# A hybrid SSM, attention and MoE block: w_out loaded during attention, and token tile 0 computed behind its split

## The chip, the cores and the metric

The kernel runs on one core of one Trainium2 chip, and its measure is the device time of one execution in microseconds. Three runs of the kernel before gave 1213.77, 1214.08 and 1216.22 us: the median is 1214.08. One more execution was profiled. It took 1210.29 us.

## The reference

The block works on 1024 tokens of 1024 channels in float32. A root-mean-square norm and one input projection give u (512 channels), q, k and v (8 heads of 64). An S5 state-space mixer turns u into y_ssm; stick-breaking attention turns q, k and v into y_att. What bears on this case comes behind both:

```
mixed = concat([rms_norm(y_ssm, g_ssm_out), rms_norm(y_att, g_attn_out)], axis=-1)   # 512 + 512 channels
x = x + mixed @ w_out                       # w_out: 1024 x 1024
h2 = rms_norm(x, g_ffn)
x = x + hierarchical_moe(h2, ...)           # 4 groups of 8 experts: the best group, its two best experts
```

rms_norm(x, g) is x / sqrt(mean(x²) + 1e-6) · g over the last axis. The MoE has 32 experts, each with a gate, an up and a down matrix (SwiGLU), 1024 x 512 or 512 x 1024.

## The kernel before, in words

**Engines and order.** Each engine (PE, DVE, ACT, POOL) and each DMA queue (SP's, ACT's, POOL's) works through its instructions in the order in which they stand; semaphores hold an instruction until what it needs is there. Outside the MoE, the scheduler of the tile framework sets that order. Buffers lie in pools on a left and a right stack of the on-chip memory, and a pool that is opened later reuses the space of one that was closed; an instruction that writes there waits for the last reader of what lay there.

**Float32 products in three passes.** A float32 operand is split into a high and a low part: `split` (L86 to L88) copies the high part on ACT (L87) and subtracts on DVE (L88). `split_mm` (L90 to L93) adds hi·hi, hi·lo and lo·hi in one PSUM bank. PSUM has 8 banks, under three tags: 3 `acc`, 2 `tr` (transposes) and 3 `m`.

**Attention.** The 8 heads go in four pairs, 8 query blocks of 128 each. For a head and a block, `att_a` makes the scores on PE (L688 to L692), a sigmoid on ACT (L693, into sb), 1 − x on POOL (L694, into bb) and a scan on DVE (L697); `att_b` transposes (L708) and copies (L712 on ACT, L714 on DVE); `att_c` multiplies with v (L721) and copies the result into q_t (L723, ACT), which by then is called oT. The scores of a pair's last block are 1024 wide, so the scans show where a pair ends and the next begins. zT, in the space of yT, holds y_ssm, transposed.

**Out projection.** Behind the attention come the small loads: gcat (the gains of both norms, SP), wr (the router's weights, L778 and L779, on ACT's queue), gpc (g_ffn, L781) and br_b (the router's bias, L784 and L785); L782 multiplies wr by gpc on DVE. Then:
- w_out in 8 row blocks of 128. Each is loaded into one of two buffers `wor` (L794, SP), scaled by gcat into wh on ACT (L795), and its low part wl made on DVE (L796). The pair is `wo[c]`.
- `row_ss` (L801 to L817), once for zT and once for oT: 8 squares of 128x512 on ACT (L806), each multiplied with a column of ones on PE (L807) to sum over the partitions; the sums are copied (L809), transposed (L812), reduced (L813), and a chain of small steps on DVE (`rstd_of`, L123 to L130, with the last copy L817) gives rs0 or rs1, one over the root of the mean square of each token. The squares have two buffers of tag h2.
- For each token tile of 128 (8 tiles): `out_open` splits the tile's zT and oT (mh, ml: L87 and L88) and loads x (L972); `out_part` makes 12 products of 128x512 for one half of the columns and one half of the rows of w_out, and adds them, scaled by rs, to x (L984 on DVE). A tile has 48 such products. `out_close` stores the result and starts the next norm on POOL; `router_turn` transposes the tile (L1009) while the next tile's products run, and `router_tile`, `norm_store` and `router_gates` do the routing.

**Expert weights.** They come in 1 MB units into a ring: 5 places rg0 to rg4 of a pool of their own (rga), then 2 in q_t, 2 in yT, and 8 more (rw) later. `load_units(n)` (L840 to L857) issues loads on SP until n units are issued; the first call, `load_units(5)`, stands behind `row_ss`. A unit whose place still holds something waits for the last reader of it. When the tiles are done, the routing is finished and the MoE's expert products begin.

The rows of the profile name lines: the products of a tile are at L91, L92 and L93 (wh·mh, wl·mh, wh·ml).

Of the kernel before, what the change touches and what calls it, by code (L numbers as in the profile page):

```python
# [8 lines left out]
F32 = mybir.dt.float32  # L9
# [3 lines left out]
AF = mybir.ActivationFunctionType  # L13
OP = mybir.AluOpType
# [4 lines left out]
D = 1024  # L19
T = 1024  # L20
NT = 8
P = 128
# [14 lines left out]
def block_kernel(ctx, tc, x, g_mix, w_in, lam_re, lam_im, log_dt, b_re, b_im, c_re, c_im, d_skip,  # L37
                 w_glu, b_glu, g_q, g_k, g_so, g_ao, w_out, g_ffn, w_rg, b_rg, w_re, b_rexp,
                 w_gate, w_up, w_down, out, dbg=None, stop=99):
    nc = tc.nc  # L40
# [3 lines left out]
    stt = nc.vector.scalar_tensor_tensor  # L44
    act = nc.scalar.activation
# [24 lines left out]
    def bank(tag):  # L70
        return banks["pool"].tile([P, 512], F32, tag=tag, bufs=banks[tag], name=tag)

    def acc():
        return bank("acc")

    def trb():
        return bank("tr")

    def mb():
        return bank("m")  # L80
# [5 lines left out]
    def split(hi, lo, src):  # L86
        nc.scalar.copy(hi, src)  # L87
        tt(lo, src, hi.bitcast(F32), op=OP.subtract)  # L88

    def split_mm(o, ah, al, bh, bl, first, last):  # L90
        mm(o, ah, bh, start=first, stop=False)  # L91
        mm(o, ah, bl, start=False, stop=False)  # L92
        mm(o, al, bh, start=False, stop=last)  # L93
# [25 lines left out]
    def rstd_of(ss, n, name, pool, eng=nc.vector):  # L119
        m = pool.tile(list(ss.shape), F32, name=name + "m", bufs=2)  # L120
        r = pool.tile(list(ss.shape), F32, name=name, bufs=2)
        t = pool.tile(list(ss.shape), F32, name=name + "t", bufs=2)
        eng.tensor_scalar(m, ss, 1.0 / n, EPS, op0=OP.mult, op1=OP.add)  # L123

        eng.tensor_scalar(r.bitcast(I32), m.bitcast(I32), -0.5, 1597463007.0, op0=OP.mult, op1=OP.add)
        for _ in range(3):
            eng.tensor_tensor(t, r, r, op=OP.mult)
            eng.tensor_tensor(t, t, m, op=OP.mult)
            eng.tensor_scalar(t, t, -0.5, 1.5, op0=OP.mult, op1=OP.add)
            eng.tensor_tensor(r, r, t, op=OP.mult)  # L130
        return r
# [497 lines left out]
    oT = [q_t[:, :, P * j:P * j + P] for j in range(4)]  # L629
    yTv = yT.rearrange("p k c t -> p k (c t)")  # L630
    zT = yTv
# [98 lines left out]
    for n in range(len(steps) + LAG + 1):  # L730
        if n < len(steps):
            h, i = steps[n]
            att_a(h, i)
        if n > LAG:
            h, i = steps[n - LAG - 1]
# [16 lines left out]
    if stop <= 2:  # L752
# [3 lines left out]


    kp = ctx.enter_context(tc.tile_pool(name="kp", bufs=1, side="right", reuse_waits="tile"))
    rga = ctx.enter_context(tc.tile_pool(name="rga", bufs=1, side="right", reuse_waits="tile"))
    late_s = ExitStack()  # L760
    late = late_s.enter_context(tc.tile_pool(name="late", bufs=1, side="left", reuse_waits="tile"))
    o3 = ExitStack()
# [2 lines left out]
    p3 = o3.enter_context(tc.tile_pool(name="p3", bufs=1, side="left", reuse_waits="tile"))  # L765
    h2d = drp.tile([T, D], F32, name="h2d")
    NE = 32
    NL = 4 + NE

    ring = [rga.tile([P, 2048], F32, name=f"rg{j}") for j in range(5)]  # L770
    ring += [q_t.rearrange("p t n -> p (t n)")[:, 2048 * j:2048 * j + 2048] for j in range(2)]
    ring += [yT.rearrange("p k c t -> p (k c t)")[:, 2048 * j:2048 * j + 2048] for j in range(2)]
    wo = [[wop.tile([P, D], FR, name=f"{nm}{c}") for nm in ("wh", "wl")] for c in range(8)]
    gcat = late.tile([P, 8], F32, name="gcat")
# [14 lines left out]
    nc.gpsimd.iota(desc, pattern=[[-1, NE]], base=NE, channel_multiplier=0,  # L789
                   allow_small_or_imprecise_dtypes=True)  # L790

    for c in range(8):
        raw = p3.tile([P, D], F32, name="wor", bufs=2)
        nc.sync.dma_start(raw, w_out[0, c * P:(c + 1) * P, :])  # L794
        act(wo[c][0], raw, AF.Copy, scale=gcat[:, c:c + 1])  # L795
        stt(wo[c][1], raw, gcat[:, c:c + 1], wo[c][0].bitcast(F32), op0=OP.mult, op1=OP.subtract)  # L796

    rs = [late.tile([P, NT], F32, name=f"rs{a}") for a in range(2)]

    def row_ss(a, src):  # L800
        ss = p3.tile([P, NT], F32, name="ssa", bufs=2)  # L801
        for hf in range(2):
            pq = acc()
            for k_ in range(4):
                sq = p3.tile([P, D], F32, name="sq3", tag="h2", bufs=2)[:, 0:512]
                act(sq, src(k_, hf), AF.Square)  # L806
                mm(pq[32 * k_:32 * k_ + 32, :], ones, sq, start=True, stop=True)  # L807
            sr = p3.tile([P, D], F32, name="sr3", tag="x2T")[:, 0:512]
            nc.scalar.copy(sr, pq)  # L809
            pt = trb()  # L810
            for t in range(4):
                nc.tensor.transpose(pt[:, t * P:(t + 1) * P], sr[:, t * P:(t + 1) * P], ident)  # L812
            nc.vector.tensor_reduce(ss[:, 4 * hf:4 * hf + 4],  # L813
                                    pt.rearrange("p (t k r) -> p t k r", t=4, k=4)[:, :, :, 0],
                                    op=OP.add, axis=AX.X)
        r = rstd_of(ss, 512, "ra", p3)
        nc.vector.tensor_copy(rs[a], r)  # L817

    row_ss(0, lambda k_, hf: zT[:, k_, 512 * hf:512 * hf + 512])
    row_ss(1, lambda k_, hf: oT[k_][:, 4 * hf:4 * hf + 4, :])  # L820


    LK = len(ring) + 8
# [8 lines left out]
    def wsrc(ap, e, half, rows):  # L832
        v = ap[0, e] if isinstance(e, int) else ap[0, bass.ds(e, 1)].squeeze(0)
        return v.rearrange("(p c) n -> p c n", p=P)[:, half * rows:(half + 1) * rows, :]
# [8 lines left out]
    def load_units(n, eng=nc.sync):  # L843

        while loaded[0] < min(n, len(units)):
            k_ = loaded[0]
            ap, s_, rows, hf = units[k_]
            e = s_
            if s_ >= NF:
                if s_ not in ev_sp:  # L850
                    ev_sp[s_] = nc.values_load(evs[0][0:1, s_:s_ + 1], engines=[mybir.EngineType.SP],
                                               min_val=0, max_val=NE - 1)
                e = ev_sp[s_]
            t_ = ring[k_ % LK]
            eng.dma_start(t_.rearrange("p (c n) -> p c n", c=rows), wsrc(ap, e, hf, rows))
            raws[k_] = t_
            loaded[0] += 1  # L857

    load_units(5)


    NS = NE - NF
# [48 lines left out]
    side = kp.tile([P, 1], F32, name="side")  # L911
# [9 lines left out]
    x2s = {}  # L921
# [4 lines left out]
        nc.gpsimd.memset(aux[:, i, :, 0], float(P * i))  # L926
    nc.vector.tensor_copy(aux[:, :, :, 1], pcol.unsqueeze(2).to_broadcast(sh))
    ET = mybir.EngineType
    pr_ = mb()[:, 0:(NT - 1) * NE].rearrange("p (i e) -> p i e", i=NT - 1)
    pr7 = mb()[:, 0:NE].unsqueeze(1)  # L930
    pc = mb()[:, 0:NE]

    def place(i, js):

# [30 lines left out]
    def out_open(i):  # L965
        mh = p3.tile([P, 8, P], FR, name="mh", bufs=2)
        ml = p3.tile([P, 8, P], FR, name="ml", bufs=2)
        tk = slice(i * P, (i + 1) * P)
        split(mh[:, 0:4], ml[:, 0:4], zT[:, :, tk])
        split(mh[:, 4:8], ml[:, 4:8], q_t[:, i, :].rearrange("p (k t) -> p k t", k=4))  # L970
        x2 = p3.tile([P, D], F32, name="xt3", bufs=2)
        nc.sync.dma_start(x2, x[0, tk, :])  # L972
        x2s[i] = dict(x2=x2, mh=mh, ml=ml, ss=p3.tile([P, 2], F32, name="ss2", bufs=2))

    def out_part(i, n, a):

        d = x2s[i]
        x2 = d["x2"]
        ns = slice(512 * n, 512 * n + 512)
        pa = acc()  # L980
        for c in range(4):
            k_ = 4 * a + c
            split_mm(pa, d["mh"][:, k_], d["ml"][:, k_], wo[k_][0][:, ns], wo[k_][1][:, ns], c == 0, c == 3)
        stt(x2[:, ns], pa, rs[a][:, i:i + 1], x2[:, ns], op0=OP.mult, op1=OP.add)  # L984
        if a:
            sq = p3.tile([P, 512], BF, name="sq2")
            act(sq, x2[:, ns], AF.Square, accum_out=d["ss"][:, n:n + 1])

    def out_close(i):
        d = x2s[i]  # L990
        nc.sync.dma_start(out[0, i * P:(i + 1) * P, :], d["x2"])
        ss = p3.tile([P, 1], F32, name="ss3", bufs=2)
        eng = nc.gpsimd
        eng.tensor_tensor(ss, d["ss"][:, 0:1], d["ss"][:, 1:2], op=OP.add)
        d["r"] = rstd_of(ss, D, "r2", p3, eng)
# [7 lines left out]
    def router_turn(i):  # L1003
        d = x2s[i]
        d["x2T"] = x2T = p3.tile([P, D], F32, name="x2T").rearrange("p (c t) -> p c t", c=8)
        for cg in range(2):
            pt = trb()
            for c in range(4):
                nc.tensor.transpose(pt[:, c * P:(c + 1) * P], d["x2"][:, 4 * cg + c::8], ident)  # L1009
            ov = x2T[:, 4 * cg:4 * cg + 4].rearrange("p c t -> p (c t)")  # L1010
            if cg:
                nc.vector.tensor_copy(ov, pt)
            else:
                nc.scalar.copy(ov, pt)
# [46 lines left out]
    def router_gates(i):  # L1061
# [7 lines left out]
        ts(o1, o1, den, None, op0=OP.mult)  # L1069
        stt(gts[:, i, :], d["o2"], e2, o1, op0=OP.mult, op1=OP.add)  # L1070

    for i in range(NT):
        out_open(i)
        out_part(i, 0, 0)
        out_part(i, 0, 1)
        if i:
            router_turn(i - 1)
        out_part(i, 1, 0)
        if i:
            router_tile(i - 1)  # L1080
            norm_store(i - 1)
            router_gates(i - 1)
        out_part(i, 1, 1)
        if i < NT - 1:
            out_close(i)
        if i == 4:
            load_units(6)
        if i >= 2:
            place(i - 2, range(i - 1))
# [482 lines left out]
    d = EX[0]  # L1572
# [160 lines left out]
```

## Time and profile before

| | |
|---|---|
| median of three runs | 1214.08 us |
| profiled execution | 1210.29 us, span 1208.6 us |
| granted TensorE clock, mean | 0.968 |
| PE busy | 1073.6 us, 89% |
| DVE busy | 632.7 us, 52% |
| ACT busy | 342.4 us, 28% |
| POOL busy | 260.5 us, 22% |
| last copy of attention (L723) begins | 445.11 us |
| transposes of token tile 0 (L1009) begin | 482.03 us |

PE is the busiest engine by far, but the share is an average: the projection and the S5 part fill it up to about 250 us, attention runs to 445, the out projection with the router to about 578, and the MoE takes the rest. A row of the windows gives, for one stretch, the busy time and the number of instructions of each engine, the granted TensorE clock (1.00 is 2.4 GHz, 0.50 is 1.2 GHz), the share of the DMA engines and what they moved. A row of the timeline gives start, duration, engine, line and operation, output <- inputs, and in brackets how long the engine stood idle before it and what ended that. A q behind an engine's name is its queue: there a DMA is issued, and the duration is that of the issue, not of the transfer.

### The profile page before, as it was taken

The page shows a single profiled execution, that of the slowest core. Times are in us where ns is not written, and L with a number is a line of the kernel's source. Part 1 is how long each engine was busy: PE and PEld are TensorE (multiplying, and loading weights), DVE is VectorE, ACT ScalarE, POOL GpSimd, SP SyncE. Part 2 cuts the span into 40 slices and gives each one's busy share as a digit, 9 for nine tenths or more (in the row PEclk, how much of TensorE's full clock was granted, in tenths as well). Part 3 has the DMA queues.
Part 4 walks back from the last instruction along what each step waited for, and adds up shares of the span by engine and source line. Part 5 has one row for each costly group of instructions (what it writes and reads, how often), then busy time and mean ns, then how long its engine had stood idle before and what let it go on. Part 6 is the DMA issues. An engine that isn't in the chain of part 4 may idle for free. (4 is left out here: it accounts for less than half of the span.)

```text
span 1208.6 us, 19739 instructions
## 1 busy us (share of the span) xinstructions
PE 1073.6 (89%) x6586; PEld 703.6 (58%) x6586; DVE 632.7 (52%) x1493; ACT 342.4 (28%) x656; POOL 260.5 (22%) x400
## 2 busy tenths in 40 slices
PE   5999999988998889999579997999799989899985
PEld 5999899985776655888334443444344444444442
DVE  6888877679787876566753222212331423322311
ACT  6325344356677654432200000000110010100011
POOL 5043113023333420222312111011120111111111
PEclk9999999998999999999689998999999999999997
DMA  7251232120000216436799999589998989999994
GB/s 258 83 112 37 42 83 54 54 88 18 2 1 1 76 53 244 155 125 226 275 349 363 358 390 384 213 281 379 399 387 331 340 301 377 371 409 391 376 390 107
DMA packets 95709, 268.45 MB, mean 222 GB/s; under 512 B 44308, under 2 KB 57432, under 8 KB 70968
## 3 DMA queue, kind: packets, MB, share of 16 engines
q1 hardware_dynamic: 80664, 232.29, 51.4%
q0 software_dynamic: 11360, 27.57, 9.1%
q10 hardware_dynamic: 3520, 6.46, 1.4%
q8 instruction: 95, 1.56, 0.5%
q14 instruction: 70, 0.57, 0.1%
HBM read 241.25 MB, written 23.86 MB: 219 GB/s over the span
## 5 line engine op out<-in xcount | busy, mean ns | idle before, releaser
L91 PE MATMUL acc<-wh,hTh 128*128 128x256 f32 x512 | 146.3, 286 | 4.2 <-ACT wh L87 4.2
L92 PE MATMUL acc<-wl,hTh 128*128 128x256 f32 x512 | 145.2, 284 | 0.0
L93 PE MATMUL acc<-wh,hTl 128*128 128x256 f32 x512 | 144.6, 282 | 0.0
L1189 POOL DMA_INDIRECT out_dram<-ysa,idx x24 | 36.7, 1530 | 314.8 <-DVE ht L1481 100.7
L91 PEld LDWEIGHTS acc<-wh,hTh 128*128 128x128 f32 x512 | 97.0, 189 | 4.8 <-ACT wh L87 4.8
L92 PEld LDWEIGHTS acc<-wl,hTh 128*128 128x128 f32 x512 | 97.0, 189 | 0.7 <-DVE wl L88 0.6
L697 DVE TENSOR_TENSOR_SCAN bb<-bb,sb 128x128 f32<-128x128 f32 (+7 forms) x64 | 89.8, 1417 | 13.7 <-POOL bb L694 13.1
L93 PEld LDWEIGHTS acc<-wh,hTl 128*128 128x128 f32 x512 | 96.9, 189 | 0.0
L694 POOL TENSOR_SCALAR bb<-sb 128x128 f32<-128x128 f32 (+7 forms) x64 | 64.8, 1016 | 95.4 <-ACT sb L693 84.1
L1457 DVE TENSOR_TENSOR hs<-hs,acc 128x512 f32<-128x512 f32 x10 | 6.9, 688 | 147.1 <-ACT hs L1453 84.4
L1210 PE MATMUL acc<-rw,xt 128*64 128x512 f32 x200 | 52.3, 616 | 10.2 <-issue 9.5
L1194 PEld LDWEIGHTS tr<-ident,xga 128*128 128x128 f32 x256 | 32.4, 195 | 44.4 <-issue 24.1
L1204 PE MATMUL acc<-rw,xt 128*128 128x512 f32 x128 | 56.9, 592 | 0.0
L1194 PE MATMUL tr<-ident,xga 128*128 128x128 f32 x256 | 38.3, 295 | 19.6 <-issue 10.0
L1452 ACT ACTIVATE hs<-acc 128x512 f32<-128x512 f32 x10 | 6.0, 597 | 171.1 <-PEq L1375 78.1
L708 PE MATMUL tr<-ident,bb 128*128 128x128 f32 x288 | 45.8, 283 | 8.4 <-DVE aT L714 3.6
L1189 POOL DMA_INDIRECT out_dram<-ysf,idx x12 | 18.8, 1567 | 158.1 <-DVE idx L1304 99.5
L91 PE MATMUL acc<-wh,mh 128*128 128x512 f32 x128 | 51.6, 405 | 0.0
L721 PE MATMUL acc<-aT,v_t 128*64 128x128 f32 x576 | 46.1, 281 | 5.8 <-DVE aT L714 4.8
L93 PE MATMUL acc<-wh,ml 128*128 128x512 f32 x128 | 50.2, 392 | 0.0
L92 PE MATMUL acc<-wl,mh 128*128 128x512 f32 x128 | 50.1, 392 | 0.0
L1455 ACT COPY hs<-acc 128x256 f32<-128x256 f32 x22 | 8.2, 373 | 147.9 <-PE acc L1210 93.8
(511 smaller groups left out, 2361.8 us busy)
## 6 DMA issues: line engine op xcount, KB each, us to landing
rw<-in_w_down_dram SPq DMA_DIRECT2D x28, 1024.0 KB
rw<-in_w_gate_dram SPq DMA_DIRECT2D x28, 1024.0 KB
rw<-in_w_up_dram SPq DMA_DIRECT2D x27, 1024.0 KB
rg<-in_w_gate_dram SPq DMA_DIRECT2D x20, 1024.0 KB
rg<-in_w_up_dram SPq DMA_DIRECT2D x20, 1024.0 KB
rg<-in_w_down_dram SPq DMA_DIRECT2D x20, 1024.0 KB
wraw<-in_w_in_dram SPq DMA_DIRECT2D x16, 512.0 KB
yT<-in_w_up_dram SPq DMA_DIRECT2D x8, 1024.0 KB
```

The costliest lines, as they stand in the source:

```text
L91: mm(o, ah, bh, start=first, stop=False)
L92: mm(o, ah, bl, start=False, stop=False)
L93: mm(o, al, bh, start=False, stop=last)
L694: nc.gpsimd.tensor_scalar(bt[:, off:T], st[:, off:T], -1.0, 1.0, op0=OP.mult, op1=OP.add)
L697: nc.vector.tensor_tensor_scan(rv, rv, sv, 0.0, op0=OP.mult, op1=OP.add)
L708: nc.tensor.transpose(pt[:, j * P:(j + 1) * P], st[:, off + (j0 + j) * P:off + (j0 + j + 1) * P], ident)
L721: mm(po[64 * r:64 * r + 64, :P], v_t[:, j, 64 * h:64 * h + 64], ATT["T", h, i][:, j, :], start=j == 0, stop=j == i)
L1189: nc.gpsimd.indirect_dma_start(out=rows, out_offset=bass.IndirectOffsetOnAxis(ap=idx[:n, :1], axis=0), in_=src[r], in_offset=None, compute ...
L1194: nc.tensor.transpose(pt[:, c], xg[:, 4 * cg + c::8], ident)
L1204: mm(p[j], xt[:, k_], hv[2 * (k_ // 4) + j][:, 512 * (k_ % 4):512 * (k_ % 4) + 512], start=k_ == 0, stop=k_ == 7)
L1210: mm(pg[r], xt[:, k_, LO], hv[2 * (k_ // 4) + j][:, 512 * (k_ % 4):512 * (k_ % 4) + 512], start=k_ == 0, stop=k_ == 7)
L1455: nc.scalar.copy(hs[:, 0:256], pg[:, 0:256])
```

## The change

It has four parts.

- The ring's pool rga moves from the right stack to the left, below the later pools. It now reuses space that is free by the last head pair, and the p3 tiles (mh, ml, wr, br_b, xt and others) come to lie where attention's buffers were until its end.
- The 8 raw row blocks of w_out are loaded into rg0 to rg3, two in each, and all are issued ahead of the split. The expert weights of those places are loaded behind the split.
- `out_first` does token tile 0 in another order: `wo_split(c)` for one row block, then its 6 products for both halves of the columns, for c = 0 to 7, in four PSUM banks that stay open (3 acc and 1 m).
- The two `row_ss` stand behind these 48 products. The squares of zT are made on POOL, with their sums in two further m banks; those of oT are made on ACT, in acc banks, which the additions of tile 0 (`out_add`) free. `load_units(5)` and three PSUM banks of the router are taken after `out_first`.

```diff
     kp = ctx.enter_context(tc.tile_pool(name="kp", bufs=1, side="right", reuse_waits="tile"))
-    rga = ctx.enter_context(tc.tile_pool(name="rga", bufs=1, side="right", reuse_waits="tile"))
+    rga = ctx.enter_context(tc.tile_pool(name="rga", bufs=1, side="left", reuse_waits="tile"))
...
+    raw = [ring[c // 2][:, D * (c % 2):D * (c % 2) + D] for c in range(8)]
     for c in range(8):
-        raw = p3.tile([P, D], F32, name="wor", bufs=2)
-        nc.sync.dma_start(raw, w_out[0, c * P:(c + 1) * P, :])
-        act(wo[c][0], raw, AF.Copy, scale=gcat[:, c:c + 1])
-        stt(wo[c][1], raw, gcat[:, c:c + 1], wo[c][0].bitcast(F32), op0=OP.mult, op1=OP.subtract)
+        nc.sync.dma_start(raw[c], w_out[0, c * P:(c + 1) * P, :])
+
+    def wo_split(c):
+        act(wo[c][0], raw[c], AF.Copy, scale=gcat[:, c:c + 1])
+        stt(wo[c][1], raw[c], gcat[:, c:c + 1], wo[c][0].bitcast(F32), op0=OP.mult, op1=OP.subtract)
...
-    def row_ss(a, src):
+    def row_ss(a, src, square, pqs):
+
         ss = p3.tile([P, NT], F32, name="ssa", bufs=2)
         for hf in range(2):
-            pq = acc()
+            pq = pqs[hf]
             for k_ in range(4):
                 sq = p3.tile([P, D], F32, name="sq3", tag="h2", bufs=2)[:, 0:512]
-                act(sq, src(k_, hf), AF.Square)
+                square(sq, src(k_, hf))
                 mm(pq[32 * k_:32 * k_ + 32, :], ones, sq, start=True, stop=True)
...
-    row_ss(0, lambda k_, hf: zT[:, k_, 512 * hf:512 * hf + 512])
-    row_ss(1, lambda k_, hf: oT[k_][:, 4 * hf:4 * hf + 4, :])
...
-    load_units(5)
...
+    def out_first():
+
+        out_open(0)
+        pa = {(n, a): acc() if n + a < 2 else mb() for a in range(2) for n in range(2)}
+        pqz = [mb(), mb()]
+        for c in range(8):
+            wo_split(c)
+            for n in range(2):
+                out_mm(0, n, c, pa[n, c // 4])
+        row_ss(0, lambda k_, hf: zT[:, k_, 512 * hf:512 * hf + 512],
+               lambda o, v: nc.gpsimd.tensor_tensor(o, v, v, op=OP.mult), pqz)
+        for n in range(2):
+            out_add(0, n, 0, pa[n, 0])
+        row_ss(1, lambda k_, hf: oT[k_][:, 4 * hf:4 * hf + 4, :], lambda o, v: act(o, v, AF.Square), [acc(), acc()])
+        for n in range(2):
+            out_add(0, n, 1, pa[n, 1])
...
+    out_first()
+    load_units(5)
```

`out_part` is cut into `out_mm` (the three products of one row block) and `out_add` (the addition and, in the second half, the square of the new x); from tile 1 on it does what it did. In the changed file the same things stand a few lines lower: wl at L799, the sums of squares at L811, their transposes at L816, the squares at L1002 (POOL) and L1005 (ACT), the router's transposes at L1029.

First place, PE behind the last products of attention (L721). Before, the sums of squares come first (tr is their transposes):

```order
L721 MATMUL acc<-aT,v_t 64x128 x16
L807 MATMUL acc<-sq_5170,ones 32x512
L807 MATMUL acc<-sq_5173,ones 32x512
L807 MATMUL acc<-sq_5176,ones 32x512
L807 MATMUL acc<-sq_5179,ones 32x512
L807 MATMUL acc<-sq_5191,ones 32x512
L812 MATMUL tr<-ident,sr_5182 128x128 x4
```

After the change, tile 0's products with row block 0 (wh_5102, wl_5103) and row block 1 stand there:

```order
L721 MATMUL acc<-aT,v_t 64x128 x16
L91 MATMUL acc<-wh_5102,mh 128x512 x2
L92 MATMUL acc<-wl_5103,mh 128x512
L93 MATMUL acc<-wh_5102,ml 128x512
L92 MATMUL acc<-wl_5103,mh 128x512
L93 MATMUL acc<-wh_5102,ml 128x512
L91 MATMUL acc<-wh_5104,mh 128x512
```

The 16 sums of squares have moved from here to behind the 48 products of tile 0; before, 14 of them stood ahead of the first of these products.

Second place, PE behind these 48 products after the change. The rows below begin with the last two of the eight sums over POOL's squares and go on to the first product of tile 1:

```order
L811 MATMUL m<-sq_5310,ones 32x512
L811 MATMUL m<-sq_5313,ones 32x512
L816 MATMUL tr<-ident,sr_5316 128x128 x4
L811 MATMUL acc<-sq_5347,ones 32x512
L811 MATMUL acc<-sq_5350,ones 32x512
L811 MATMUL acc<-sq_5353,ones 32x512
L811 MATMUL acc<-sq_5356,ones 32x512
L811 MATMUL acc<-sq_5367,ones 32x512
L816 MATMUL tr<-ident,sr_5359 128x128 x4
L811 MATMUL acc<-sq_5370,ones 32x512
L91 MATMUL acc<-wh_5102,mh 128x512
```

The sums over ACT's squares go into acc banks, which tile 0's first two additions have to free, and tile 1's products stand behind six of them. Until tile 0's transposes (L1009, after: L1029) PE has done 72 products of tiles 0 and 1 before the change and 79 after it.

Third place, DVE behind attention. Before, the first low part of w_out stands ahead of the product of the router's weights (L782):

```order
L917 TENSOR_TENSOR sided<-side,sideq 128x1
L796 SCALAR_TENSOR_TENSOR wl_5103<-wor,gcat,wh_5102 128x1024
L782 TENSOR_TENSOR wr<-wr,gpc 128x288
L796 SCALAR_TENSOR_TENSOR wl_5105<-wor,gcat,wh_5104 128x1024
L813 TENSOR_REDUCE ssa<-tr 128x4
```

After the change, L782 stands between the two halves of tile 0's ml split, ahead of all eight low parts:

```order
L88 TENSOR_TENSOR ml<-yT,mh 128x512
L782 TENSOR_TENSOR wr<-wr,gpc 128x288
L88 TENSOR_TENSOR ml<-q_t,mh 128x512
L799 SCALAR_TENSOR_TENSOR wl_5103<-rg_5097,gcat,wh_5102 128x1024
L799 SCALAR_TENSOR_TENSOR wl_5105<-rg_5097,gcat,wh_5104 128x1024
```

The splits of tiles 0 and 1 (four times L88) stood within the last head pair before. On ACT, the issues of wr and br_b, which stood there too, now follow the last L723, ahead of the first split.

## Rows read from the trace of the kernel before

**Rows 1.** Windows by stage: stretch, length, busy time of each engine, clock, DMA.

```profile
445.00:464.00 19.00, 13.99 (x45) 3.62 (x45) 9.98 (x29) 15.60 (x24) 0.00 (x0) 1.00 0.75 268
482.00:578.00 96.00, 95.27 (x547) 81.02 (x546) 60.28 (x217) 31.63 (x75) 22.97 (x106) 1.00 0.47 170
600.00:1208.00 608.00, 537.29 (x2535) 245.00 (x2531) 176.80 (x455) 55.13 (x118) 92.13 (x70) 0.96 0.93 346
```

**Rows 2.** Timeline behind attention: start, duration, engine, line, operation, idle time before.

```profile
445.11 0.27 ACT L723 COPY q_t<-acc 128x128 f32<-128x128 f32 x1 [2.05 <-PE acc L721]
445.12 0.36 ACTq L781 DMA_DIRECT2D gpc<-in_g_ffn_dram  x1
...
450.63 0.46 DVE L782 TENSOR_TENSOR wr<-wr,gpc 128x288 f32<-128x288 f32 x1 [2.63 <-DMA gpc<-in_g_ffn_dram]
```

**Rows 3.** Timeline of PE ahead of and at tile 0's transposes.

```profile
477.26 0.39 PE L91 MATMUL acc<-wh,mh 128*128 128x512 f32 x1
...
481.80 0.40 PE L93 MATMUL acc<-wh,ml 128*128 128x512 f32 x1
482.03 1.04 PE L1009 MATMUL tr<-ident,xt 128*128 128x128 f32 x8
```

**Rows 4.** Timeline of DVE at two turns of head pairs, and ACT's issue.

```profile
362.93 2.29 DVE L697 TENSOR_TENSOR_SCAN bb<-bb,sb 128x1024 f32<-128x1024 f32 x1 [0.95 <-POOL bb L694]
...
380.00 0.76 DVE L600 SCALAR_TENSOR_TENSOR K<-tr,gqk,K 64x512 fp32r<-64x512 f32 x1
380.79 1.49 DVE L697 TENSOR_TENSOR_SCAN bb<-bb,sb 128x640 f32<-128x640 f32 x1
...
400.29 0.09 DVE L787 MEMSET ones<- 128x32 f32 x1
...
401.21 2.37 DVE L697 TENSOR_TENSOR_SCAN bb<-bb,sb 128x1024 f32<-128x1024 f32 x1
...
420.76 1.48 DVE L697 TENSOR_TENSOR_SCAN bb<-bb,sb 128x640 f32<-128x640 f32 x1
...
400.55 4.08 ACTq L784 DMA_DIRECT2D br_b<-in_b_router_group_dram  x1
```

**Rows 5.** Groups by line, 380 to 520 us: busy time, mean ns, idle before.

```profile
L796 DVE SCALAR_TENSOR_TENSOR wl<-wor,gcat,wh 128x1024 fp32r<-128x1024 f32 x8 | 10.3, 1282 | 5.5 <-ACT wh L795 5.5
L795 ACT ACTIVATE wh<-wor,gcat 128x1024 fp32r<-128x1024 f32 x8 | 9.0, 1143 | 2.3 <-DMA wor<-in_w_out_dram 2.2 <-issue 0.2
L806 ACT ACTIVATE sq<-q_t 128x512 f32<-128x512 f32 x8 | 4.7, 620 | 0.6 <-PE acc L807 0.6
L88 DVE TENSOR_TENSOR ml<-q_t,mh 128x512 fp32r<-128x512 f32 x6 | 4.5, 757 | 0.0
L809 ACT COPY sr<-acc 128x512 f32<-128x512 f32 x4 | 2.3, 576 | 2.9 <-PE acc L807 2.9
```

**Rows 6.** Instructions of line 565 on POOL: duration min/median/max, ns.

```profile
L565 POOL TENSOR_TENSOR v_t<-v_t,vp x4: 1256/1267/1272, 264.9 to 270.5; 128x512 f32<-128x512 f32 x4
```

**Rows 7.** Timeline of DVE at tile 0's first addition and rs1's chain.

```profile
469.02 0.74 DVE L984 SCALAR_TENSOR_TENSOR xt<-acc,rs,xt 128x512 f32<-128x512 f32 x1
469.68 0.16 DVE L123 TENSOR_SCALAR ram<-ssa 128x8 f32<-128x8 f32 x1
...
472.31 0.17 DVE L130 TENSOR_TENSOR ra<-ra,rat 128x8 f32<-128x8 f32 x1
```

**Rows 8.** Timeline of PE: two products behind long idle times.

```profile
269.99 0.55 PE L688 MATMUL m<-K,QH 128*128 128x256 f32 x1 [3.59 <-DVE ql L600]
...
1036.01 1.50 PE L1210 MATMUL acc<-rw,xt 128*64 128x512 f32 x6 [3.22 <-issue]
```

**Rows 9.** Windows behind these idle times, and one of full PE.

```profile
270.00:278.00 8.00, 3.87 (x14) 2.83 (x14) 7.49 (x17) 7.11 (x10) 4.31 (x7) 0.50 0.20 61
856.00:862.00 6.00, 5.89 (x36) 3.01 (x37) 3.17 (x5) 0.28 (x1) 1.74 (x2) 0.72 1.02 392
1036.00:1038.00 2.00, 1.99 (x10) 0.96 (x11) 0.00 (x0) 0.00 (x0) 0.00 (x0) 1.00 1.05 311
```

More of the change, by code (lines that the diff above doesn't have):

```diff
@@ L928, in block_kernel @@
     ET = mybir.EngineType
-    pr_ = mb()[:, 0:(NT - 1) * NE].rearrange("p (i e) -> p i e", i=NT - 1)
-    pr7 = mb()[:, 0:NE].unsqueeze(1)
-    pc = mb()[:, 0:NE]
     def place(i, js):
@@ L973, in out_open, with out_mm, out_add @@
         x2s[i] = dict(x2=x2, mh=mh, ml=ml, ss=p3.tile([P, 2], F32, name="ss2", bufs=2))
-    def out_part(i, n, a):
+    def out_mm(i, n, c, pa):
+        d = x2s[i]
+        ns = slice(512 * n, 512 * n + 512)
+        split_mm(pa, d["mh"][:, c], d["ml"][:, c], wo[c][0][:, ns], wo[c][1][:, ns], c % 4 == 0, c % 4 == 3)
+    def out_add(i, n, a, pa):
         d = x2s[i]
@@ L979, in out_part @@
         ns = slice(512 * n, 512 * n + 512)
[L980 to L983, printed above, removed]
         stt(x2[:, ns], pa, rs[a][:, i:i + 1], x2[:, ns], op0=OP.mult, op1=OP.add)
@@ L987, in out_part @@
             act(sq, x2[:, ns], AF.Square, accum_out=d["ss"][:, n:n + 1])
+    def out_part(i, n, a):
+        pa = acc()
+        for c in range(4 * a, 4 * a + 4):
+            out_mm(i, n, c, pa)
+        out_add(i, n, a, pa)
+    def out_first():
[13 more added lines that the diff above has]
+            out_add(0, n, 1, pa[n, 1])
     def out_close(i):
@@ L1070, in router_gates @@
         stt(gts[:, i, :], d["o2"], e2, o1, op0=OP.mult, op1=OP.add)
+    out_first()
+    load_units(5)
+    pr_ = mb()[:, 0:(NT - 1) * NE].rearrange("p (i e) -> p i e", i=NT - 1)
+    pr7 = mb()[:, 0:NE].unsqueeze(1)
+    pc = mb()[:, 0:NE]
     for i in range(NT):
-        out_open(i)
-        out_part(i, 0, 0)
-        out_part(i, 0, 1)
         if i:
+            out_open(i)
+            out_part(i, 0, 0)
+            out_part(i, 0, 1)
             router_turn(i - 1)
-        out_part(i, 1, 0)
-        if i:
+            out_part(i, 1, 0)
             router_tile(i - 1)
@@ L1082, in block_kernel @@
             router_gates(i - 1)
-        out_part(i, 1, 1)
+            out_part(i, 1, 1)
         if i < NT - 1:
```

## The prediction, made before the changed kernel ran

> **What bounds the kernel now.** I read the windows by stage first, then the timeline around the end of attention, then the groups by line for what one instruction costs. In the windows [rows 1] the reader is to look at PE's busy time against the length of each stretch. From 482 to 578 us PE is busy for 95.27 of 96 us at full clock: the token tiles' products with w_out and the router follow each other without a gap, so there a delay of PE passes on whole. From 445 to 464 it is busy for only 13.99 of 19 us. That is where the change works: the stretch between the last copy of attention, 445.11 [rows 2], and the transposes of token tile 0 for the router, 482.03 [rows 3]. I call them A and B. Before, A to B is 36.92 us.
>
> After B every engine's instructions stand in the same order in both kernels. The MoE that follows holds its DMAs at 0.93 [rows 1], and I first looked whether a late start could vanish there. Its stream stops at places of the ring that become free only by expert products, and those wait for the last tile's routing; so a shift of B comes out at the end whole, unless the last rival is right.
>
> **The change part by part.**
>
> *Attention gets lighter.* Before, the p3 tiles lie where tile 0 and 1's halves mh and ml can be split during the last head pair, and ACT issues the small router loads there. One of these issues, L784, held ACT for 4.08 us, beside two loads of w_out and two of x [rows 4]. After, all of that stands behind attention. To price it I compare the turn from one head pair to the next. From the 1024-wide scan that opens the last turn (401.21) to the 640-wide scan (420.76) are 19.55 us; from 362.93 to 380.79, one turn earlier, 17.86, which hold two scalings of K, 0.76 each, that the last turn hasn't [rows 4]. So the last turn is 19.55 − (17.86 − 1.52) = 3.2 us too long, and 0.92 us of DVE work on constants ahead of it (400.29 to 401.21), which stands earlier after the change, makes 4.1. Bounds: 2.9 if that work is paid earlier instead and the issues of eight 512 KB loads cost a little, 5.5 if the 4.08 us go whole and most of the splits too; 8.1 would need the ACT stall, the four ml splits (0.8 each [rows 5]) and the constants to have been in line. I take −4.1. Loading w_out there costs nothing by itself: the eight loads (4 MB) are issued by SP with no one waiting behind them until A, some 40 us later.
>
> *A to the end of tile 0's 48 products.* After A, ACT issues five small loads. An issue that nothing holds takes 0.36 (gpc's [rows 2]) or a little more; I take 2.4 for the five. Then come mh of zT and of oT, 0.6 each as ACT's other copies of this size, and the wh splits at 1.14 [rows 5]: wh0 is there at A + 4.75, the others follow every 1.1. DVE has the ml split, then wr × gpc (L782), then the second ml, then the wl splits at 1.28 [rows 5]. L782 is the added wait: it stands ahead of ml and all eight wl, and PE waits for these. The bounds: DVE comes to it at A + 3.8, and gpc is issued third, at about A + 1.2; before, gpc's load took from 445.12 until its use at 450.63, 5.5 us, beside a 1 MB load [rows 2], which would be A + 6.7. The x loads that are queued on SP wait for scans some ten us earlier, so the queues are nearly empty; but two loads of 1024 pieces each go ahead of gpc on its queue. I take A + 5.2, between both. Then L782 (0.46) and ml (0.7) end at 6.35 and wl0 at 7.65. PE does two products at 4.75, waits 2.4 us, and from then on has six products a row block at 0.227 (20 steps from 477.26 to 481.80 [rows 3]), 1.365 us, which is just longer than a wl split: PE is the slower one, and the 48 products end at 7.65 + 0.9 + 7 × 1.365 = A + 18.1. By the bounds of L782's wait it is 17.2 to 19.6.
>
> *From there to B.* Two of POOL's eight squares of zT are made in attention's end; the other six wait for a buffer that only PE's use of an earlier square frees, and in PE's order these uses stand behind the 48 products. POOL takes 1.27 us for a 128x512 product of two operands [rows 6], 1.33 with the hand-over: the last is used at 9.1 behind the products. Then one after the other: ACT's copy 0.6, transposes 0.7, the reduce, rs0's chain of 15 small DVE steps at 0.20 (469.68 to 472.31 holds 13 of them [rows 7]), which makes 13.8, and the addition at 0.74 [rows 7] that frees an acc bank: 14.55. Only then may the first ACT square be multiplied, since its product goes into that bank. PE has nothing from 10.5 to 14.6. Five squares at 0.65 (ACT's square is 0.62 [rows 5], with two buffers) and a row of transposes lead to 18.9; tile 1's first 31 products (7.0) and three square products (1.6) to 27.5. rs1's chain and its two additions come to 27.8 as well. So B stands at 27.8 behind the 48 products.
>
> Before, B has 72 products of tiles 0 and 1 behind it, after the change 79: 7 more, 1.6 us, are done already. A to B after is 18.1 + 27.8 − 1.6 = 44.3 against 36.92: +7.4 at full clock. It is longer though the idle time at its start is shorter, because before, the squares' products and the chains of rs lie beside the weight split, and now they stand behind it, in a line, with POOL at twice ACT's time for a square.
>
> *The clock.* PE's idle time now comes in longer pieces: 4.7 us broken by nothing at A and 2.4 more behind two products, then 4.1 ahead of the ACT squares. In the trace an idle time of 3.59 us was followed by the level of 1.2 GHz: 0.50 for all of 270 to 278, with PE busy for half of it [rows 8, 9]. An idle time of 3.22 was not: 1.00 in 1036 to 1038 [rows 8, 9]. Where PE is full while the clock is low, 856 to 862 has a mean of 0.72, so 3.4 of 6 us were at half speed, and 1.7 us of work was lost [rows 9]. The first gap, ahead of a full stream, costs that: +1.7. The second is followed by five products that come at ACT's pace, during which a low clock lasts as in 270 to 278, and then by the full stream: 1.7 and about 1.0 for the products and transposes in the line, +2.7. Together +4.4.
>
> The trace speaks here with a rule of the Trainium skill, "TensorE: Matmul & The Clock Gate", section "HAM oscillation — how this bites in real kernels": matmuls that come in bursts with waits between them put the array back to the low clock, so that each burst begins cold. It speaks against a change that lets PE run behind a split and then wait for a chain; by that rule both gaps cost, and without it the sum would be 4.4 less. The 3.59 and 3.22 us here agree with it only as far as two cases can.
>
> *The sum.* 7.4 − 4.1 + 4.4 = +7.7. The profiled execution took 1210.29 us (span 1208.6), so it would take 1218.0; the runs have a median of 1214.08, 3.79 above, so a median of 1221.8. The bounds of the parts: L782 −0.9 to +1.5, attention −5.5 to −2.9, the clock 0 to +5.
>
> **The rivals.**
>
> *The clock holds* in one or both gaps. For it: 3.22 us held, and two products and some transposes stand between the idle pieces. Against: 4.1 and 4.7 are longer than any that held. The time is 1221.8 − 4.4 = 1217.4 with both, about 1219.5 with one.
>
> *Attention gives back as much as the tail loses.* The other side of no change: if ACT's stall, the ml splits and the constants were all in line, the last turn is 8.1 us shorter, and with a held clock the sum is 7.4 − 8.1 = −0.7, with gpc landing early −1.6: 1212.5 to 1213.4. For it: DVE hardly pauses in the last pair. Against: ACT was late by the 4.08 of L784 while DVE went on with its 2.37 us scan [rows 4], so the two overlap. It decides if the 640-wide scan starts 7 us or more ahead of where it did.
>
> *The small loads hold ACT again.* L778, L779 and a third issue now stand ahead of ACT's splits; if the third waits for the queue as L784 did, 4.08 us come on top, and everything behind A with them: about 1225.9. For it: the same two loads of small pieces stood ahead of it then. Against: the 2 MB of x and w_out beside it are gone.
>
> *The shift is swallowed later:* the weight stream of the MoE, not the tiles, sets the end. DMA's 0.93 speaks for it, the stop of the stream at the ring's last place against it. The time would be that of before, 1214 to 1216.
>
> **How the numbers follow.** The forecast has 0.47; the held clock 0.25; the even trade 0.10; the held issue 0.10; the swallowed shift 0.08. Faster or slower means by more than 0.2%, 2.4 us, what a measurement can tell from nothing. The forecast, the held issue and most of the held clock are slower: 0.78. The swallowed shift and half of the even trade and a little of the held clock are no change: 0.16. An even trade with more luck is faster: 0.06. The range of 8 in 10 goes from 1214.0 to 1226.0; the forecast's own is 1219.5 to 1224.
>
> **What would show it.** Right: the 640-wide scan about 4 us early; wh0 some 4.7 us behind the last attention copy; six POOL squares in a row behind the last wl split with PE mostly idle; L1029's first transposes about 45 us or more behind A; a granted clock below 0.9 in the stretch. Wrong: POOL's squares done before the 48 products end, tile 1's products ahead of the ACT squares, L782 in line for nothing, or routing that starts no later than before.

## The result, and the profile after

The changed kernel takes 1229.31 us, the median of four runs (1228.60 to 1232.00), against 1213.92 for the kernel before (four runs, the three shown above and one more). The ratio is 1.0124, with a 95% interval of 1.0102 to 1.0146: by it 15.1 us slower. The prediction had the sign, and 7.7 us; its range ended at 1226.0. The profiled execution took 1228.60 us (span 1226.9), 18.3 more than that of before.

The stretches between fixed points tell where this is. S is the second 1024-wide scan of the last turn of head pairs, A the last copy of attention, B tile 0's transposes for the router, M the first transposes of the MoE. Each line is read from one profile:

| us | S | S to A | A to B | B to M | M to end |
|---|---|---|---|---|---|
| before | 401.21 | 43.90 | 36.92 | 110.57 | 616.00 |
| after | 402.54 | 44.23 | 54.08 | 109.33 | 616.72 |
| predicted change | | −4.1 | +13.4 | −1.6 | 0 |
| measured change | +1.33 | +0.33 | +17.16 | −1.24 | +0.72 |

Before S both kernels have the same instructions, save a few constants, and most of the 1.3 us is there from the start: line 565 on DVE, which stands well ahead of anything changed, begins at 257.2 us before and at 258.3 after, and at 258.0 to 259.3 in four of the kernels below (the early load, the sums ahead, two squares to a buffer, the loads on SP). The profile of before had begun a little early. What the change does is in A to B, and attention gave next to nothing back.

The timeline of DVE at the turn of head pairs, after, answers to [rows 4], and behind it stand two rows of ACT:

```profile
364.24 2.29 DVE L697 TENSOR_TENSOR_SCAN bb<-bb,sb 128x1024 f32<-128x1024 f32 x1 [0.76 <-POOL bb L694]
382.12 1.49 DVE L697 TENSOR_TENSOR_SCAN bb<-bb,sb 128x640 f32<-128x640 f32 x1
402.54 2.37 DVE L697 TENSOR_TENSOR_SCAN bb<-bb,sb 128x1024 f32<-128x1024 f32 x1 [0.88 <-POOL bb L694]
...
409.10 0.27 ACT L723 COPY q_t<-acc 128x128 f32<-128x128 f32 x1 [4.53 <-PE acc L721]
...
446.77 0.27 ACT L723 COPY q_t<-acc 128x128 f32<-128x128 f32 x1 [2.05 <-PE acc L721]
```

The last pair has lost its small loads and its four ml splits, and is as long as before. ACT now idles for 4.53 us where L784 had held it for 4.08 [rows 4]: it waits for PE, and PE for DVE. The timeline of PE there, after, and behind it the clock in windows (stretch, length, busy time of PE, PEld, DVE, ACT and POOL, clock, DMA share, GB/s; PEld is PE's loading of weights):

```profile
405.41 0.55 PE L708 MATMUL tr<-ident,bb 128*128 128x128 f32 x3 [1.46 <-DVE aT L714]
406.32 2.74 PE L721 MATMUL acc<-aT,v_t 128*64 128x128 f32 x26 [0.37 <-DVE aT L714]
...
425.80 1.09 PE L721 MATMUL acc<-aT,v_t 128*64 128x128 f32 x16 [2.25 <-DVE aT L714]
```

The second and the third of these rows in the kernel before:

```profile
405.68 1.74 PE L721 MATMUL acc<-aT,v_t 128*64 128x128 f32 x26
...
422.87 1.09 PE L721 MATMUL acc<-aT,v_t 128*64 128x128 f32 x16 [0.94 <-DVE aT L714]
```

And the windows, after:

```profile
404.00:406.00 2.00, 0.55 (x3) 0.31 (x3) 2.00 (x4) 0.57 (x1) 1.00 (x1) 1.00 1.00 395
408.00:410.00 2.00, 2.00 (x14) 1.57 (x12) 0.49 (x1) 0.41 (x2) 0.00 (x0) 0.50 0.98 406
```

DVE is full from 404 to 406 with the scan and the copies behind it, and PE has 0.55 us of work; then PE works at 1.2 GHz, and its 26 products take 2.74 us (1.74 before). This low clock is not the change's alone: two of the kernels below leave the ml splits in the last pair, as before, and have it at the same place (the small loads on SP, POOL's squares in the kernel before). S to A is 44.38 and 44.43 us in them. It is 44.14 to 44.23 in the four profiles of the changed order with the clock low there and nowhere else up to A (after, the early load, the first with the gaps filled, the fastest). So with the clock alike, the lighter last pair gave 0.2 to 0.3 us.

Later DVE does two 640-wide scans ahead of a copy (L714) that stood between them before. Its timeline, after; the row of three scans holds both:

```profile
419.84 5.32 DVE L697 TENSOR_TENSOR_SCAN bb<-bb,sb 128x512 f32<-128x512 f32 x3
425.08 0.66 DVE L714 COPY aT<-tr 128x512 f32<-128x512 f32 x1
```

The first of the two begins at 421.20, which is 18.66 us behind S, 0.9 sooner than before (19.55). But the copy begins 22.54 us behind S, where it was 20.95, and PE waits 2.25 us for it (0.94 before).

Behind A, the timeline of PE, after, which answers to [rows 3]; then ACT's and DVE's first rows there, which answer to [rows 2]:

```profile
452.07 1.22 PE L91 MATMUL acc<-wh,mh 128*128 128x512 f32 x2 [5.34 <-ACT wh L798]
453.39 0.79 PE L92 MATMUL acc<-wl,mh 128*128 128x512 f32 x1
...
465.93 0.39 PE L93 MATMUL m<-wh,ml 128*128 128x512 f32 x1
466.25 1.05 PE L811 MATMUL m<-sq,ones 128*32 128x512 f32 x4
...
471.25 1.05 PE L811 MATMUL m<-sq,ones 128*32 128x512 f32 x2 [0.18 <-POOL sq L1002]
...
476.81 0.66 PE L816 MATMUL tr<-ident,sr 128*128 128x128 f32 x4 [0.73 <-ACT sr L813]
481.56 1.92 PE L811 MATMUL acc<-sq,ones 128*32 128x512 f32 x4 [4.09 <-DVE xt L980]
484.25 2.43 PE L811 MATMUL acc<-sq,ones 128*32 128x512 f32 x4 [0.77 <-ACT sq L1005]
486.88 1.92 PE L811 MATMUL acc<-sq,ones 128*32 128x512 f32 x2 [0.20 <-ACT sq L1005]
...
500.85 1.15 PE L1029 MATMUL tr<-ident,xt 128*128 128x128 f32 x8 [0.39 <-DVE xt L980]
```

```profile
448.86 0.44 ACTq L784 DMA_DIRECT2D br_b<-in_b_router_group_dram  x1
...
449.83 0.62 ACT L87 CAST mh<-yT 128x512 fp32r<-128x512 f32 x1 [2.80 <-DMA wr<-in_w_router_group_dram]
450.87 8.43 ACT L798 ACTIVATE wh<-rg,gcat 128x1024 fp32r<-128x1024 f32 x8
...
451.09 0.45 DVE L782 TENSOR_TENSOR wr<-wr,gpc 128x288 f32<-128x288 f32 x1
```

ACT's five issues take 2.8 us, L784's 0.44 of them, and L782 waits for nothing. Tile 0's 48 products end at 466.16, 19.4 us behind A; then come zT's sums at POOL's pace, and PE's idle 4.09 us for rs0 and tile 0's addition, exactly where the prediction had it. The windows of PE there, after, and one that answers to the second of [rows 1]:

```profile
452.00:456.00 4.00, 3.83 (x8) 2.63 (x9) 4.00 (x5) 4.00 (x5) 0.00 (x0) 0.50 0.18 29
458.00:466.00 8.00, 8.00 (x37) 6.53 (x35) 4.91 (x6) 2.33 (x4) 0.00 (x0) 0.99 1.01 380
478.00:482.00 4.00, 0.44 (x2) 0.18 (x4) 3.52 (x16) 0.00 (x0) 0.00 (x0) 0.57 0.00 0
482.00:486.00 4.00, 3.23 (x8) 0.36 (x4) 0.16 (x1) 1.15 (x2) 0.00 (x0) 0.50 0.00 0
500.85:592.50 91.65, 91.23 (x518) 77.23 (x519) 57.49 (x207) 31.68 (x77) 22.89 (x105) 1.00 0.48 173
```

The clock is low behind both gaps. From B on PE is full, as before, so what A to B lost is not given back.

### The profile page after: what moved, and what is told of

Its sections match the earlier page's. It is cut to its first block, busy times and chain, and to the rows that moved or that the text cites. A ratio compares the mean times of both kernels' runs of the same rounds, so it can differ in the third digit from the quotient of the medians.

```text
span 1226.9 us, 19727 instructions
## 1 busy us (share of the span) xinstructions
PE 1081.7 (88%) x6586; PEld 705.4 (57%) x6586; DVE 631.4 (51%) x1493; ACT 337.9 (28%) x648; POOL 273.0 (22%) x408
## 5 line engine op out<-in xcount | busy, mean ns | idle before, releaser
L1218 PE MATMUL tr<-ident,xga 128*128 128x128 f32 x256 | 38.3, 295 | 19.4 <-issue 9.8
L721 PE MATMUL acc<-aT,v_t 128*64 128x128 f32 x576 | 46.3, 284 | 6.7 <-DVE aT L714 5.5
```

The lines of the kernel that those rows point to most:

```text
L721: mm(po[64 * r:64 * r + 64, :P], v_t[:, j, 64 * h:64 * h + 64], ATT["T", h, i][:, j, :], start=j == 0, stop=j == i)
L1218: nc.tensor.transpose(pt[:, c], xg[:, 4 * cg + c::8], ident)
```

## Experiments

Ratios are against runs of the kernel before on the same chip, with 95% intervals. The edits are shown shortened: `...` and words such as `zT or oT` or `POOL's square` stand for what the kernels write out.

**The early load alone.** Both sums are made on ACT ahead of tile 0, `out_first` is left out, and tile 0 goes through the loop of the other tiles, as before.

```diff
-    out_first()
+    for c in range(8):
+        wo_split(c)
+    for a in range(2):
+        row_ss(a, zT or oT, lambda o, v: act(o, v, AF.Square), [acc(), acc()])
```

> The early load and the moved pool alone: raw w_out comes into the ring places during attention, but both sums of squares are made on ACT ahead of tile 0, and tile 0 is computed as in the kernel before. Theory S (the changed kernel loses because squares, their sums and the chains of rs stand in a line behind tile 0's products): the stretch from the last attention copy A to tile 0's router transposes B is 35 to 40 us instead of 54.1, and the time lies between 1 us below and 4 us above the kernel before; what is left is the later end of attention, some 1.7 us. Rival L (it loses because the halves, the small loads and constants no longer stand in the last head pair): A to B stays above 44 and the time is 8 us or more above before.

Measured: 1.0092 (1.0059 to 1.0124), A to B 48.1. S as I had put it falls short: the sums stand ahead of the products, and the kernel is slow. The timelines of PE and ACT say why:

```profile
458.51 2.44 PE L811 MATMUL acc<-sq,ones 128*32 128x512 f32 x4 [12.10 <-ACT sq L829]
```

```profile
449.52 8.42 ACT L798 ACTIVATE wh<-rg,gcat 128x1024 fp32r<-128x1024 f32 x8 [2.80 <-DMA wr<-in_w_router_group_dram]
457.85 1.14 ACT L829 ACTIVATE sq<-yT 128x512 f32<-128x512 f32 x2
```

With all of w_out there at A, nothing holds ACT's eight splits back, and they run ahead of the squares: PE waits 12.1 us. Before, two raw buffers held them back: two splits began at 445.53, the third only at 453.75, behind seven squares. Both numbers are those that were put down for L, but L is not the cause, since with the same moved work the next kernel is fast.

**The sums ahead of tile 0's products,** all else as in the changed kernel.

```diff
+        row_ss(0, zT, POOL's square, [mb(), mb()])
+        row_ss(1, oT, ACT's square, [mb(), mb()])
         pa = {...}
         for c in range(8):
             wo_split(c)
             ...
-        row_ss(0, ...); out_add(...); row_ss(1, ...); out_add(...)
+        out_add(...) four times
```

> The changed kernel with both sums of squares called ahead of tile 0's products (squares of zT on POOL, of oT on ACT, their sums in m banks); tile 0 still follows the split row block by row block. Theory S: the sums lie beside the split again, A to B is 36 to 41 us, the time is at most 4 us above before. Rival L: 8 us or more above before. A third reading, that following the split row block by row block is itself slow (PE at 1.36 us a row block, low clock at the start): A to B stays above 46.

Measured: 0.9971 (0.9956 to 0.9987), A to B 35.15. The layout, the early load and the following of the split all stay, and 19 of the 54 us go. So the price is that the sums stand behind the products, where nothing else is left for PE. The edit also takes the sums over oT's squares out of the acc banks, and so out of their wait for rs0; the kernel with banks of their own, below, prices that part by itself.

**Two squares to a buffer.**

```diff
-                sq = p3.tile([P, D], F32, name="sq3", tag="h2", bufs=2)[:, 0:512]
+                if k_ % 2 == 0:
+                    sq2x = p3.tile([P, D], F32, name="sq3", tag="h2", bufs=2)
+                sq = sq2x[:, 512 * (k_ % 2):512 * (k_ % 2) + 512]
```

> The changed kernel with two squares in each of the two buffers, so that four squares can be under way and PE can take two sums at once. Theory S with the buffer hand-over as its main price: POOL makes four squares before the products end, the last of zT's sums comes 2 to 4 us earlier, oT's sums go in pairs, and the time falls by 4 to 7 us against the changed kernel. Rival (the chains of small DVE steps and the low clock are the price, not the buffers): less than 2 us.

Measured: 1.0065 (1.0045 to 1.0086), A to B 47.59, 6.5 less than after (7.2 by the ratios): what was put down for the hand-over, at its upper end. Its timeline shows what a sum costs PE. The rows are four sums together (a sum is two passes), then one:

```profile
466.20 1.07 PE L813 MATMUL m<-sq,ones 128*32 128x512 f32 x8
468.97 1.04 PE L813 MATMUL m<-sq,ones 128*32 128x512 f32 x2 [1.71 <-POOL sq L1004]
```

Four take 1.07 us and one takes 1.04. The wait for rs0 is still there, 4.09 us.

**ACT's issues taken away from the kernel before.** The five small loads are issued by SP.

```diff
-    nc.scalar.dma_start(wr[:, :, 0:4], ...)   # and the four others
+    nc.sync.dma_start(wr[:, :, 0:4], ...)
```

> The kernel before with the five small router loads issued by SP instead of ACT; the rest of the order in attention is nearly the same. If the issue that held ACT for 4.08 us was in line with attention's end, as the prediction had it, the last turn of head pairs (1024-wide scan to 640-wide scan, 19.55 us) becomes 2 to 4 us shorter and the time falls by as much. If it was hidden behind DVE's scan and POOL: within 1 us.

Measured: 0.9990 (0.9974 to 1.0007). The turn, from the timeline of DVE:

```profile
402.89 2.36 DVE L697 TENSOR_TENSOR_SCAN bb<-bb,sb 128x1024 f32<-128x1024 f32 x1
422.92 1.48 DVE L697 TENSOR_TENSOR_SCAN bb<-bb,sb 128x640 f32<-128x640 f32 x1
```

20.03 us, against 19.55 [rows 4]: with L784's 4.08 us gone from ACT the turn is no shorter. The stall was hidden but for some 0.6 us: PE's 26 products begin 3.84 us behind S, where they began at 4.47, and then take 2.75 us instead of 1.74. The window there has the low clock:

```profile
408.00:410.00 2.00, 2.00 (x16) 1.57 (x14) 0.20 (x2) 0.27 (x1) 0.00 (x0) 0.50 0.12 36
```

**PE kept at work in its gaps.** 16 small products behind A, 15 ahead of the sums over oT's squares; their results go nowhere.

```diff
+        for j in range(16):
+            mm(pa[0, 0][:, 0:P], ident, oT[3][:, 7, :], start=True, stop=True)
         for c in range(8):
...
+        trb()
+        fill = trb()
+        for j in range(15):
+            mm(fill, wo[0][0][:, 0:P], wo[0][1][:, 0:512], start=True, stop=True)
```

> The changed kernel with PE kept at work in its two gaps by products whose results are thrown away: 16 small ones behind attention's last copy, ahead of tile 0's products, and 15 ahead of the sums over oT's squares. Nothing real starts earlier by it. If the low clock behind the gaps is part of the loss, the granted clock stays at 1.00 through the stretch, tile 0's 48 products end some 2 us earlier and the sums over oT's squares run in 1.05 us each in place of 1.92: 3 to 6 us below the changed kernel. If the waits alone are the loss: within 1.5 us of it.

Measured: 1.0120 (1.0088 to 1.0152), A to B 49.31. The window over that stretch, and rows of PE from the first of the sums over oT's squares to the transposes behind the fifth:

```profile
446.47:495.78 49.31, 42.09 (x174) 24.46 (x175) 23.45 (x58) 19.56 (x29) 6.70 (x6) 1.00 0.27 89
```

```profile
479.09 1.05 PE L811 MATMUL acc<-sq,ones 128*32 128x512 f32 x4 [0.65 <-DVE xt L980]
...
482.68 1.05 PE L811 MATMUL acc<-sq,ones 128*32 128x512 f32 x2 [0.20 <-ACT sq L1011]
483.66 0.66 PE L816 MATMUL tr<-ident,sr 128*128 128x128 f32 x4
```

The clock is 1.00 throughout, a single sum there takes 1.05 instead of 1.92, and the stretch is 4.8 us shorter with every real wait left in. But the time hardly fell, so the same kernel was measured once more:

> The changed kernel with both gaps of PE filled, once more and in more rounds, since its profile showed 5.0 us gained up to the start of the MoE and its runs only 1.2. If the gain is real and the MoE's own scatter hid it: the median lies 3 to 6 us below the changed kernel. If the MoE gives it back: 0 to 2 us below, and the profile again shows 3 us more in the MoE.

Measured: 1.0113 (1.0087 to 1.0140), A to B 50.90, and M to end 622.5 (620.0 in the first) against 616.7 after. This time the products in the first gap didn't hold the clock: it is 0.50 in 456 to 458, among tile 0's products, and the stretch is only 3.2 us shorter. In these two profiles, then, the fill gave back 3.2 us of A to B with the low clock in one gap's wake, and 4.8 without any. M to end lies between 614.9 and 622.5 over all the profiles, in no order that I see: it was 620.6 with two squares to a buffer and 620.9 in the fastest kernel. That the gain comes out at the end is not shown, and whether the fill lengthens the MoE stays open.

**zT's squares on ACT** in the changed kernel: `act(o, v, AF.Square)` in place of POOL's product.

> The changed kernel with zT's squares made on ACT instead of POOL, still behind the 48 products. If POOL's time for a square (1.27 us and more against ACT's 0.62) sets the pace of zT's sums, the stretch from the end of the products to rs0 becomes 2 to 4 us shorter, and so does the time against the changed kernel. If PE's single sums (1.05 us each, two buffers) set it: less than 1.5 us.

Measured: 1.0110 (1.0085 to 1.0135), A to B 52.01. In the profile 2.1 us of the stretch are POOL's slower squares (the longest wait between zT's sums is 0.71 where it was 1.72); the runs don't tell it from nothing.

**The sums over oT's squares in banks of their own,** so that they don't wait for rs0 and tile 0's additions.

```diff
-        pa = {...}
         pqz = [mb(), mb()]
+        pa = {...}
...
-        row_ss(1, ..., [acc(), acc()])
+        row_ss(1, ..., [mb(), mb()])
```

> The changed kernel with the sums over oT's squares in the m banks that the sums over zT's have left, so that they wait for no acc bank and so not for rs0's chain and tile 0's additions. The prediction priced that wait at 4.1 us, and behind it the low clock at 2.7. If that holds: PE has no idle time of 4 us there, the clock stays at 1.00 behind it, and the stretch from A to B falls from 54.1 to 46 to 49 us, the time by 4 to 8. If something else lies in line in its place: less than 2.

Measured: 1.0045 (1.0025 to 1.0066), A to B 43.92, 10.2 us less than after. The timeline of PE there shows the last transposes of zT's sums and then the first sums over oT's squares:

```profile
479.29 0.66 PE L816 MATMUL tr<-ident,sr 128*128 128x128 f32 x4 [0.53 <-ACT sr L813]
479.88 1.51 PE L811 MATMUL m<-sq,ones 128*32 128x512 f32 x4
481.64 1.56 PE L811 MATMUL m<-sq,ones 128*32 128x512 f32 x4 [0.26 <-ACT sq L1005]
```

No gap, and the clock is 1.00 from here to B. Two sums take 1.5 us there, where a single one took 1.92. This one wait and what hung on it is the largest piece of the loss: 9.6 of the 15.1 us by the ratios.

**POOL's squares in the kernel before**, the rest as it was.

> The kernel before with nothing changed but that zT's squares are made on POOL, which is idle behind attention, instead of ACT, which is busy for 15.6 of the 19 us there. If ACT sets the pace of the stretch, A to B becomes 2 to 4 us shorter and the time falls by as much. If POOL's squares are late or slow DVE's splits (in the run with the squares ahead, DVE's wl took 1.91 beside POOL's squares against 1.28): no change or up to 3 us slower.

Measured: 1.0041 (1.0014 to 1.0067). A to B is 39.05, 2.1 longer: PE waits 2.5 us for POOL's squares, and behind that the clock is 0.50 in 452 to 454. Two of POOL's squares also stand ahead of a 1 − x in attention, and the second 1024-wide scan begins 4.59 us behind the first, where it was 3.16. B to the last tile's transposes is 97.5 us there against 92.2: PE waits 1.82 us for ACT's copy of tile 0, and then the clock is low again. Whether that hangs on the squares is not shown.

**The sums ahead, and the small loads on SP.**

> The kernel with the sums called ahead of tile 0's products, and the five small router loads issued by SP instead of ACT, so that ACT's first split begins some 2.8 us earlier behind attention. If the ACT issues are in line: A to B falls by 1 to 3 us from 35.1, the time as much. If PE's sums are what the stretch waits for at its start: less than 1 us.

Measured: 0.9996 (0.9982 to 1.0010), A to B 37.08. Taking the issues from ACT gained nothing once PE has sums to do. That A to B is 1.9 longer than with the sums ahead alone stays open; fewer of its sums come in pairs.

**The sums ahead, two squares to a buffer:** the two edits above together.

> The kernel with the sums ahead of tile 0's products, with two squares in each of the two buffers. If the sums hold PE so long because most come singly (1.05 us each, while two at once take 1.05 together), the 16 sums end some 4 us earlier, A to B falls from 35.1 to 30 to 33 us and the time to 3 to 8 us below the kernel before. If PE is then held by the split instead (ACT's wh stand among the squares): A to B 34 to 36, the time as with the sums ahead alone.

Measured: 0.9938 (0.9923 to 0.9953), 1209.66 us: faster than both kernels, by the ratio about 7.5 us under the one before. A to B is 31.06, with PE hardly idle and at full clock (the window begins 0.13 us ahead of A):

```profile
446.60:477.79 31.19, 29.36 (x121) 16.82 (x121) 23.23 (x59) 19.76 (x31) 4.67 (x5) 1.00 0.43 145
```

## Why the prediction was wrong

The direction was right, and so was the mechanism behind A; the size was half of what was measured, and two steps failed.

*"Attention gets lighter", −4.1: this step failed.* S to A is 43.9 to 45.7 us in all thirteen profiles, with the small loads and splits inside or outside, 43.90 before and 44.23 after; with the clock alike, the change gave 0.2 to 0.3 us. I compared one turn with another, put the difference down to ACT's held issue and the ml splits, and took them off. The run with SP's issues showed that ACT was hardly in line. By the traces PE was: it waited for DVE's scan and copy in either case, and after the change it waited longer for the copy that the scheduler had moved behind a scan, which took back the 0.9 us gained up to the 640-wide scan. No run tests the place of that copy by itself. The rival that I priced at 8.1 us of gain rested on the same reading and fell with it; its own counter-argument, that DVE's scan went on while ACT was held, was the right one.

*From the products to B, 27.8 at full clock and 2.7 for the clock: 34.7 in fact.* Up to the moment when rs0 frees the banks it held: 15.4 us against 14.55. Behind it, 19.29 us against 13.25 and the 2.7. The mis-sized term is a sum's price on PE. I took 0.65 us for each of oT's five, ACT's pace, but a sum that comes by itself takes PE 1.05 at full clock, which the trace of the kernel before already showed in its timeline of PE:

```profile
450.05 1.05 PE L807 MATMUL acc<-sq,ones 128*32 128x512 f32 x2 [0.20 <-ACT sq L806]
```

The five took 7.17 us at the low clock (481.56 to 488.73), 4.57 with the gap filled and the clock at 1.00 (479.09 to 483.66), and 3.25 in my sum. The three that stand among tile 1's products, 1.6 us in all by my sum, took 1.04 each. So of the 4.2 us that were missing here, some 2.8 are the sums with the waits between them, at full clock: an estimate from these rows. The run with banks of their own prices the wait and all that hangs on it at 10.2 us of the stretch, where I had 6.8.

*Right within 1 us:* A to the end of the 48 products (19.8 predicted with the clock, 19.4 measured; luck in part, since ACT's issues took 2.8 and not 2.4, L782's wait of 1.4 was not there, and the errors cancelled); PE's 4.1 us of idle time (4.09); the low clock behind both gaps; the seven products given back (1.24 of 1.6); the delay passing on whole. By stretches: −4.1 against +0.3, +13.4 against +17.2, and 1.3 us that lay in the start of the profile of before. The rival of a held issue did not happen, nor did the clock hold. The Trainium skill's page "TensorE: Matmul & The Clock Gate" states in "HAM oscillation — how this bites in real kernels" that waits between bursts of matmuls bring the low clock back. This trace bore it out twice: 5.34 us of idle time and then 0.50 in 452 to 456, 4.09 and then 0.50 in 482 to 486. A low clock came without such a gap too: 0.50 in 408 to 410 after the change, behind idle times of 1.46 and 0.37 us, where the kernel before had 1.99 and 0.39 and kept 1.00. I had left that out of account.

## What to carry to other kernels

When a preparation on ACT or DVE paces PE, look at what else PE can do meanwhile, and leave that work in front: sums and chains that were cover there became a line of their own when they were moved behind. A bank that the next step needs ties it to the chain that frees it; a bank of its own was worth 10 us of the stretch here. A stall that an engine shows is worth nothing until the trace says that the engine others wait for was waiting for it. And before a stretch of one profile is set against that of another, see where the clock was low in each.

## What was not expected of the hardware

- A sum over partitions (32 columns of ones, four of them to different rows of one bank) takes PE 1.04 us alone and 1.07 for four together, when all four squares are there.
- DVE beside POOL's squares, in the kernel with the sums ahead, from its timeline:

```profile
453.55 1.29 DVE L782 TENSOR_TENSOR wr<-wr,gpc 128x288 f32<-128x288 f32 x1
454.76 1.52 DVE L88 TENSOR_TENSOR ml<-q_t,mh 128x512 fp32r<-128x512 f32 x1
456.36 1.91 DVE L799 SCALAR_TENSOR_TENSOR wl<-rg,gcat,wh 128x1024 fp32r<-128x1024 f32 x1
```

  They took 0.46, 0.69 and 1.28 in the kernel before, without POOL at work. The Trainium skill's "GPSIMD Engine Reference", section "1. Specifications", says that the two engines share their interfaces to the on-chip memory, and the rows agree with it.
- The end of attention, with the same order on DVE and ACT, took 1.5 us longer in some executions than in others (S to A 45.70 with the sums ahead, 44.21 with two squares to a buffer as well). In the first the clock was low twice, 0.57 in 425 to 429 and in 442 to 446 us; in the second once, 0.63 in 406 to 410.
